# Weight sums of the output product's first half made one by one in earlier pairs and kept in DRAM

## The chip, the cores and the metric

The kernel runs on one core of a Trainium2 chip. The core has a matrix engine (TensorE, called PE in the profile; PEld is its weight load), a vector engine (VectorE, DVE), an activation engine (ScalarE, ACT), a general one (GpSimd, POOL) and a queue engine (SyncE, SP), which here issues nearly all transfers between DRAM and the on-chip buffers. Each engine runs its instructions in a fixed order and waits at each for what it needs.

The metric is device time in microseconds. The kernel before takes 1977.21 us, the median of three runs (1974.11 to 1977.57).

## The reference, cut to what matters

One decoder layer on 512 tokens of width 2048, in float32:

```python
h = rms_norm(x, norm1_g)
proj = h @ w_in                      # columns for two groups of heads
out_a = gla_mixer(...)               # 4 heads, chunked gated linear attention
out_b = dilated_mixer(...)           # 8 heads, dilated windows, QK-norm, T5 bias
mix = concatenate([out_a, out_b], -1)
x = x + mix @ w_out                  # the output product
h2 = rms_norm(x, norm2_g)
x = x + (silu(h2 @ w_gate) * (h2 @ w_up)) @ w_down
```

The change concerns how the weights of `mix @ w_out` are prepared, for the first 1024 of its 2048 columns.

## The kernel before

**Products by pairs.** Every large product is made in pairs of two 512-column blocks, `w1` and `w2`, for all 512 tokens. A pair splits the depth into four groups of 512 rows (three in the last down projections) and works by a scheme with seven products instead of eight (Winograd's form of Strassen's): the weights of a group come as four quarters of 256 rows by 512 columns, `a` and `c` from `w1`, `b` and `d` from `w2`. The seven products, in the order P1, P5, P6, P3, P7, P2, P4 (`PRODUCTS`), use `a`, `d` and `c` as they are (P1, P3, P2: `SINGLE`) and four sums: P5 is b - a, P6 is d minus that, P7 is d - b, P4 is c minus the P6 sum (`SUMS_OF`). The other operand has its own sums (A11, S1 and so on, made by `Operand.split` and the jobs around it).

**One item.** A product of one group is an item; a pair has 28. `stream` (the loop around lines 315 to 370) goes through the items of all pairs. For the item after the next, `Pair.source` gives the weights: a quarter loaded from DRAM (`load_quarter`, line 222), or a sum that DVE makes in place from two quarters (line 256). Each weight tile is then split in a high part `wh`, rounded by ACT (line 331), and a low part `wl`, the rest, made by DVE (line 335). PE does 12 matmuls an item (line 361): eight with `wh` against the operand's high and low parts, four with `wl`. Two buffers each hold `wh` and `wl`, twelve buffers of 512 KB hold weight quarters (tag `w`). A quarter in use for a later sum keeps its buffer; a load waits until one is free.

**Beside the items.** After the first eight matmuls of each item the pair's `step` runs some of the background: work written as generators, a piece at each `yield`. In the pairs of the input product these are the gates, the bias tables (a copy of 2.5 MB within DRAM, `rep_d`) and the attention heads, which read the projections back from DRAM. During the output product's first pair, `late_jobs` makes that product's remaining operand sums from `mix_d` (the mixers' output in DRAM): a load of 256 KB into one of the buffers T, v, qT, kT or r, a DVE subtraction or addition (lines 1242 to 1246) and a split (lines 174 and 175). `rate` and `paced` say how much a step runs.

**Order.** PE, ACT and DVE follow the order of the program in the first pair, which is written out by hand. In the others a planner orders the instructions of each engine, and the issues on SP's queue, by program order among those that its own estimate of time holds ready; so a sum may be placed ahead of the point at which it is written, where it expects DVE to be idle. What was placed is then fixed, and an instruction whose data come late holds up what stands behind it on its engine.

**The pairs in question.** The hand-ordered pair (`first_pair`) is pair 1. The list `pairs` holds the rest: pairs 2 to 5 are the input product's further columns (va1/va0, qb0/kb0, vb1/vb0, qb1/kb1), pair 6 the gate, pairs 7 and 8 the two halves of the output product (`opm`), then eleven pairs for the SwiGLU's inputs and six for its output.

The buffers with tag `r` (four of 256 KB, `rpool`) hold parts of x in pair 1 and are used again by the heads of the dilated mixer and by the operand jobs.

Of the kernel before, what the change touches and what calls it, by code (L numbers as in the profile page):

```python
# [10 lines left out]
F32 = mybir.dt.float32  # L11
# [3 lines left out]
ALU = mybir.AluOpType  # L15
# [3 lines left out]
P = 128  # L19
# [14 lines left out]
SINGLE = {"P1": "a", "P3": "d", "P2": "c"}  # L34
SUMS_OF = {"P5": "ba", "P6": "da", "P7": "db", "P4": "ca"}
# [72 lines left out]
def block_kernel(ctx: ExitStack, tc: tile.TileContext, ins, out):  # L108
# [127 lines left out]
    class Pair:  # L236


        def __init__(self, op, rows, w1, w2, final, step, scale=None, before=None):
            self.op, self.rows, self.w1, self.w2 = op, rows, w1, w2  # L240
            self.final, self.step, self.scale, self.before = final, step, scale, before
            self.q, self.dst, self.held = {}, {}, {}

        def quarter(self, name, g):
# [5 lines left out]
        def source(self, prod, g):  # L250

            if prod in SINGLE:
                return self.quarter(SINGLE[prod], g)
            one, two = SUMS_OF[prod]
            src = self.quarter(two, g)
            nc.vector.tensor_tensor(src, self.quarter(one, g), src, op=ALU.subtract)  # L256
            return src
# [50 lines left out]
        def end(self, prod):  # L308
            src = self.dst[prod]
            if prod in ("P1", "P5", "P6"):  # L310
                self.held[prod] = self.seeds(src, int(prod == "P5"))
            elif prod == "P4":
                later(1, lambda: self.final(1, 0, None, src), hold=True)
            else:
                which = {"P3": "P6", "P7": "P5", "P2": "P1"}[prod]
                self.close(self.held[which], src, *CLOSES[prod])

    def stream(pairs):

# [173 lines left out]
        later(1, lambda: close("d"), hold=True)  # L493

    background = []
    deferred = []

    def later(units, fn, hold=False):
# [22 lines left out]
    def finish(ready):  # L521

        while not ready():
            run_soon()
            try:
                next(background[0])
            except StopIteration:
                background.pop(0)

    def paced(counts):  # L530
        counts = iter(counts)
        return lambda: step(next(counts, 1))

    def rate(*stretches):


        owed = [0.0]
        rates = iter([r for n, r in stretches for _ in range(n)])

        def go():  # L540
            owed[0] += next(rates, stretches[-1][1])
            n = owed[0] if owed[0] > 0.3 else 0
            owed[0] = min(owed[0] - (step(n) or 0.0), 1.0)

        return go
# [546 lines left out]
    def final_proj(n1, n2):  # L1092
        def final(half, which, tiles, acc_):
            if tiles is None:
                tiles = emitted(acc_, lambda m: row_scale(half, m))
            name = (n1, n2)[which]
            dst = proj[name]
            for m in range(2):
                r = half * 256 + m * P
                put = lambda r=r, m=m: store(dst[r : r + P, :], tiles[m])  # L1100
                if name[:2] in ("qb", "kb"):
                    heads_norm(tiles[m], put)
                else:
# [184 lines left out]
    def pair(*args, **kw):  # L1288
        pairs.append(Pair(*args, **kw))

    pair(opx, rows_in, col(1536), col(1024), final_proj("va1", "va0"), rate((22, 1), (6, 0.6)),
         row_scale, before=lambda: background.extend([gates(), bias_tables()]))
    flow = rate((90, 0.41))
    pair(opx, rows_in, col(3088), col(4112), final_proj("qb0", "kb0"), flow, row_scale)
    pair(opx, rows_in, col(5648), col(5136), final_proj("vb1", "vb0"), flow, row_scale)
    pair(opx, rows_in, col(3600), col(4624), final_proj("qb1", "kb1"), flow, row_scale)
    pair(opx, rows_in, col(2048), col(2560), final_gate, rate((5, 0.6), (23, 1.05)), row_scale)


    rows_mix = [(1024 + 256 * g, 256 * order[g]) for g in range(4)]  # L1300
# [36 lines left out]
    def final_out(second):  # L1337
        rest_of = {}

        def ahead(half, which):  # L1340
            tok = 1 - half
            rest_of[half, which] = residual_loads(
                [2 * tok, 2 * tok + 1], 512 * (2 * second + which),
                lambda t, c: x[t * P : (t + 1) * P, c : c + 512],
            )

        def final(half, which, tiles, acc_):
            tok = 1 - half
            rows = [2 * tok, 2 * tok + 1]
            ch = 2 * second + which  # L1350
            tiles = residual(tiles, acc_, rest_of.pop((half, which)))
            for m in range(2):
                t = rows[m]
                store(x1_d[t][:, 512 * ch : 512 * ch + 512], tiles[m])
                jk = work("st", (P, DV), bufs=2).bitcast(mybir.dt.bfloat16)
                nc.scalar.activation(
                    jk, tiles[m], AF.Square, accum_out=ss2[:, t, ch : ch + 1]
                )
            if second:
                turn = scaled_store(tiles, rows, tok, xn_d[2 * ch : 2 * ch + 2], 4 * ch)  # L1360

                def rest():
                    turn()
                    if which == 1 and half == 1:
                        background.append(early_jobs(opn, (2, 3), tops, False))
                        background.append(late_jobs(opn, ((2, 3),), tops, bots, False))

                later(2, rest)
                if which == 0 and half == 1:
                    output_scales()  # L1370
            elif which == 0 and half == 1:
                nc.vector.tensor_tensor(part2, ss2[:, :, 0], ss2[:, :, 1], op=ALU.add)
# [35 lines left out]
        turn()  # L1408
        yield

    ocol = lambda c: w_out[:, c : c + 512]
# [190 lines left out]
```

## Time and profile before

| | us |
|---|---|
| median of three runs | 1977.21 |
| the profiled execution, device time | 1975.93 |
| its span (first to last instruction) | 1974.1 |
| PE busy | 1932.0 |
| DVE busy | 1655.0 |
| ACT busy | 1094.1 |

How to read it: the page gives for each engine its busy time, its share of the span and its instructions. A table of windows gives the same for stretches of the span, with the clock that PE was granted (1.00 is full), the mean busy share of the 16 DMA engines and what they moved. A timeline line has the start in us, the duration, the engine, the line of the kernel, the operation with what it writes and reads, the count of what was merged into the line, and in brackets the idle time of the engine before it with what ended it. Matmuls overlap, so a merged line's duration reaches into the next one's start; the pace is read from starts. A line of transfers gives their count, their size and the median time from issue to landing.

### The profile page before, as it was taken

Reading aid. Unit: us, or ns where it says so; the run is one execution under the profiler, and the core shown is the slowest. Engines: PE = TensorE matmul, PEld = TensorE weight load, DVE = VectorE, ACT = ScalarE, POOL = GpSimd, SP = SyncE. Lnnn points to the kernel's source line nnn. Section 1 sums busy time; section 2 is a strip of 40 time slices with the busy share of each in tenths; the row PEclk is TensorE's granted clock in tenths of the full one; section 3 lists DMA queues with packets and bytes.
Section 4 is the critical chain, followed back from the end, with each engine's and each line's share of the span. In section 5 each row is a group of like instructions: output and inputs, shape, how many; then the busy total and the mean of one; then the engine's idle time right before and its main releaser. Section 6 shows DMA issues by size and latency. Waiting matters only on the chain.

```text
span 1974.1 us, 25791 instructions
## 1 busy us (share of the span) xinstructions
PE 1932.0 (98%) x9226; PEld 1671.6 (85%) x9226; DVE 1655.0 (84%) x1850; ACT 1094.1 (55%) x1600; POOL 58.7 (3%) x81
## 2 busy tenths in 40 slices
PE   7999999999999999999999999999999999999998
PEld 6888888888878877888888888888888888888887
DVE  7997887868789789878878878878879989989987
ACT  6664564566766666545545545445446646546443
POOL 0000230010000000000000000000000000000000
PEclk9999999999999999999999999999999999999999
DMA  8358365374666685554554554554555855855762
GB/s 277 113 170 276 106 186 157 127 213 133 214 205 203 215 278 163 179 166 129 182 166 132 176 165 129 175 163 132 172 163 168 294 204 180 301 179 178 248 213 75
DMA packets 237113, 360.45 MB, mean 183 GB/s; under 512 B 18246, under 2 KB 96783, under 8 KB 236984
## 3 DMA queue, kind: packets, MB, share of 16 engines
q1 hardware_dynamic: 236776, 358.72, 57.3%
q8 instruction: 72, 1.18, 0.3%
q14 instruction: 57, 0.47, 0.1%
q10 hardware_dynamic: 208, 0.08, 0.0%
HBM read 296.59 MB, written 64.51 MB: 183 GB/s over the span
## 4 chain that ended last, share of the span: by engine, by line
PE 79%; DVE 8%; DMA 7%; issue 3%; ACT 2%; SPq 1%; POOL 1%; DVEq 0%; ACTq 0%
PE acc L361 71%; DVE wl L335 3%; PE acc L429 3%; DVE wa L256 1%; PE bank L1120 1%; PE bank L978 1%; ACT wh L331 1%; DMA wc<-in_w_in 1%; DVE AS L175 1%; DMA T<-p_d 1%; DMA x<-in_x 1%; DMA q<-y_d 0%; PE bank L1010 0%; DMA xn_d<-oT 0%; DVE seed L1325 0%
## 5 line engine op out<-in xcount | busy, mean ns | idle before, releaser
L361 PE MATMUL acc<-wh,AS 128*128 128x512 f32 x3008 | 712.0, 379 | 0.0
L361 PEld LDWEIGHTS acc<-wh,AS 128*128 128x128 f32 x3008 | 569.1, 189 | 81.7 <-ACT wh L331 0.6
L331 ACT CAST wh<-wa 128x1024 fp32r<-128x1024 f32 x376 | 393.6, 1048 | 384.2 <-PE acc L361 359.5
L361 PE MATMUL acc<-wh,AA 128*128 128x512 f32 x2256 | 536.4, 381 | 5.6 <-ACT wh L331 5.4
L335 DVE TENSOR_TENSOR wl<-wa,wh 128x1024 fp32r<-128x1024 f32 x376 | 457.4, 1220 | 72.0 <-ACT wh L331 46.5
L361 PEld LDWEIGHTS acc<-wh,AA 128*128 128x128 f32 x2256 | 426.7, 190 | 70.0 <-ACT wh L331 9.1
L361 PE MATMUL acc<-wl,AS 128*128 128x512 f32 x1504 | 395.7, 386 | 7.9 <-DVE wl L335 7.2
L361 PEld LDWEIGHTS acc<-wl,AS 128*128 128x128 f32 x1504 | 278.9, 189 | 61.7 <-DVE wl L335 20.9
L361 PE MATMUL acc<-wl,AA 128*128 128x512 f32 x1128 | 299.0, 388 | 6.1 <-DVE wl L335 6.1
L361 PEld LDWEIGHTS acc<-wl,AA 128*128 128x128 f32 x1128 | 210.7, 190 | 38.7 <-DVE wl L335 9.0
L331 ACT CAST wh<-wb 128x1024 fp32r<-128x1024 f32 x94 | 98.6, 1049 | 127.4 <-PE acc L361 122.7
L331 ACT CAST wh<-wc 128x1024 fp32r<-128x1024 f32 x94 | 98.4, 1047 | 106.8 <-PE acc L361 102.2
L331 ACT CAST wh<-wd 128x1024 fp32r<-128x1024 f32 x94 | 98.4, 1048 | 105.8 <-PE acc L361 102.3
L256 DVE TENSOR_TENSOR wa<-wc,wa 128x1024 f32<-128x1024 f32 x94 | 114.6, 1223 | 43.8 <-DMA wc<-in_w_gate 24.2
L335 DVE TENSOR_TENSOR wl<-wc,wh 128x1024 fp32r<-128x1024 f32 x94 | 114.8, 1221 | 38.6 <-ACT wh L331 38.6
L335 DVE TENSOR_TENSOR wl<-wd,wh 128x1024 fp32r<-128x1024 f32 x94 | 114.5, 1220 | 35.0 <-ACT wh L331 28.1
L335 DVE TENSOR_TENSOR wl<-wb,wh 128x1024 fp32r<-128x1024 f32 x94 | 113.9, 1219 | 6.1 <-ACT wh L331 6.1
L256 DVE TENSOR_TENSOR wb<-wd,wb 128x1024 f32<-128x1024 f32 x94 | 114.6, 1219 | 1.0 <-DMA wd<-in_w_in 0.5
L256 DVE TENSOR_TENSOR wa<-wb,wa 128x1024 f32<-128x1024 f32 x94 | 113.7, 1220 | 0.8
L256 DVE TENSOR_TENSOR wa<-wd,wa 128x1024 f32<-128x1024 f32 x94 | 113.1, 1218 | 0.1
L298 DVE SCALAR_TENSOR_TENSOR seed<-acc,rs,seed 128x512 f32<-128x512 f32 x96 | 70.5, 746 | 24.9 <-PE acc L361 24.9
L282 ACT ACTIVATE seed<-acc,rs 128x512 f32<-128x512 f32 x96 | 60.6, 681 | 1.4 <-PE acc L361 0.8
(289 smaller groups left out, 1367.4 us busy)
## 6 DMA issues: line engine op xcount, KB each, us to landing
wa<-in_w_gate SPq DMA_DIRECT2D x44, 512.0 KB, 4.4
wb<-in_w_up SPq DMA_DIRECT2D x44, 512.0 KB, 4.4
wd<-in_w_up SPq DMA_DIRECT2D x44, 512.0 KB, 4.5
wc<-in_w_gate SPq DMA_DIRECT2D x44, 512.0 KB, 3.6
wc<-in_w_in SPq DMA_DIRECT2D x28, 512.0 KB, 4.1
wa<-in_w_in SPq DMA_DIRECT2D x24, 512.0 KB, 5.2
wb<-in_w_in SPq DMA_DIRECT2D x24, 512.0 KB, 6.1
wd<-in_w_in SPq DMA_DIRECT2D x24, 512.0 KB, 6.0
```

The lines of the kernel that those rows point to most:

```text
L175: nc.vector.tensor_tensor(a[:, :, 1, :], src, a[:, :, 0, :].bitcast(F32), op=ALU.subtract)
L256: nc.vector.tensor_tensor(src, self.quarter(one, g), src, op=ALU.subtract)
L282: nc.scalar.activation(halves(t), unfolded(src[m]), AF.Copy, scale=self.scale(half, m))
L298: nc.vector.scalar_tensor_tensor(halves(seed[m]), unfolded(src[m]), self.scale(half, m), halves(seed[m]), op0=ALU.mult, op1=ALU.add,)
L331: nc.scalar.copy(high[k], sources[k])
L335: nc.vector.tensor_tensor(low[k], sources.pop(k), high[k].bitcast(F32), op=ALU.subtract)
L361: nc.tensor.matmul(p.dst[prod][m], a[:, jj, hl, m * P : (m + 1) * P], folded(w[:, jj, :]), start=fresh and g == 0 and len(terms) == 2 and ...
L429: recent["pe"] = nc.tensor.matmul(dst[prod][m], a[:, jj, hl, m * P : (m + 1) * P], folded(w[:, jj, :]), start=fresh and g == 0 and len(ter ...
L978: nc.tensor.matmul(lp[:, :n], qh[:, b * P : (b + 1) * P], kh[:, :n], start=True, stop=True)
L1120: nc.tensor.transpose(bk[:, jj, m * P : (m + 1) * P], tiles[m][:, f : f + P], ident)
```

## The change: sums from DRAM

A new generator, `weight_sums`, makes the four sums of pair 7 for each of its four groups, in halves of 128 rows: eight rounds. A round loads four parts of 128x512 (256 KB) into the `r` buffers, waits four steps, makes one subtraction in each of the next four steps, then stores four results to DRAM tiles (`out_sums`) and rests two steps. It is advanced by one piece in every step of pairs 2, 3 and 4 (`beside`), beside the background that these steps run anyhow. A round takes ten steps, the whole 80 of the 84 steps of these pairs.

In pair 7, `source` loads each sum as one tile of 512 KB. It has 28 weight loads instead of 16, seven a group instead of four, makes no sum on DVE and keeps no quarter past its own product.

```diff
@@ class Pair
+            self.sums = sums
@@ def source(self, prod, g)
             if prod in SINGLE:
-                return self.quarter(SINGLE[prod], g)
+                t = self.quarter(SINGLE[prod], g)
+                if self.sums:
+                    self.q.pop((SINGLE[prod], g))
+                return t
+            if self.sums:
+                t = wpool.tile([P, 2, 512], F32, name=nm("ws"), tag="w")
+                load(t, self.sums[prod, g])
+                return t
             one, two = SUMS_OF[prod]
...
+    def weight_sums(rows, w1, w2, sums):
+
+        tt = nc.vector.tensor_tensor
+
+        def fetch(g, j):
+            res = []
+            for name in "abdc":
+                r0 = rows[g][0 if name in "ab" else 1] + P * j
+                t = rpool.tile([P, 2, 256], F32, name=nm("r"), tag="r").rearrange(
+                    "p a b -> p (a b)")
+                load(t, (w1 if name in "ac" else w2)[r0 : r0 + P, :])
+                res.append(t)
+            return res
+
+        for g in range(4):
+            for j in range(2):
+                a, b, d, c = fetch(g, j)
+                for _ in range(4):
+                    yield
+                for dst, one, two in (
+                    (a, b, a), (b, d, b), (d, d, a), (c, c, d)
+                ):
+                    tt(dst, one, two, op=ALU.subtract)
+                    yield
+                for prod, t in (("P5", a), ("P7", b), ("P6", d), ("P4", c)):
+                    store(sums[prod, g][:, j, :], t)
+                yield
+                yield
...
+    aside = []
...
+    def side(units):
+
+        count = [0]
+
+        def go():
+            count[0] += 1
+            if aside and count[0] % units == 0:
+                try:
+                    next(aside[0])
+                except StopIteration:
+                    aside.pop(0)
+
+        return go
+
+    def both(*fns):
+        return lambda: [fn() for fn in fns]
...
+    ocol = lambda c: w_out[:, c : c + 512]
+    rows_mix = [(1024 + 256 * g, 256 * order[g]) for g in range(4)]
+    out_sums = {
+        (prod, g): dram([P, 2, 512], f"{prod}_{g}_d") for prod in SUMS_OF for g in range(4)
+    }
+    aside.append(weight_sums(rows_mix, ocol(0), ocol(512), out_sums))
+    beside = side(1)
-    pair(opx, rows_in, col(1536), col(1024), final_proj("va1", "va0"), rate((22, 1), (6, 0.6)),
+    pair(opx, rows_in, col(1536), col(1024), final_proj("va1", "va0"),
+         both(rate((22, 1), (6, 0.6)), beside),
          row_scale, before=lambda: background.extend([gates(), bias_tables()]))
     flow = rate((90, 0.41))
-    pair(opx, rows_in, col(3088), col(4112), final_proj("qb0", "kb0"), flow, row_scale)
-    pair(opx, rows_in, col(5648), col(5136), final_proj("vb1", "vb0"), flow, row_scale)
+    flowing = both(flow, beside)
+    pair(opx, rows_in, col(3088), col(4112), final_proj("qb0", "kb0"), flowing, row_scale)
+    pair(opx, rows_in, col(5648), col(5136), final_proj("vb1", "vb0"), flowing, row_scale)
     pair(opx, rows_in, col(3600), col(4624), final_proj("qb1", "kb1"), flow, row_scale)
...
-    pair(opm, rows_mix, ocol(0), ocol(512), final_out(0), paced([1] * 28),
+    pair(opm, rows_mix, ocol(0), ocol(512), final_out(0), paced([1] * 28), sums=out_sums,
          before=lambda: finish(lambda: ("S3", 3) in opm.t))
     pair(opm, rows_mix, ocol(1024), ocol(1536), final_out(1), rate((28, 1.2)))
```

More of the change, by code (lines that the diff above doesn't have):

```diff
@@ L236, in block_kernel, with __init__ @@
     class Pair:
-        def __init__(self, op, rows, w1, w2, final, step, scale=None, before=None):
+        def __init__(self, op, rows, w1, w2, final, step, scale=None, before=None, sums=None):
             self.op, self.rows, self.w1, self.w2 = op, rows, w1, w2
             self.final, self.step, self.scale, self.before = final, step, scale, before
+            self.sums = sums
             self.q, self.dst, self.held = {}, {}, {}
@@ L1289, in pair @@
         pairs.append(Pair(*args, **kw))
-    pair(opx, rows_in, col(1536), col(1024), final_proj("va1", "va0"), rate((22, 1), (6, 0.6)),
+    ocol = lambda c: w_out[:, c : c + 512]
[7 more added lines that the diff above has]
+         both(rate((22, 1), (6, 0.6)), beside),
          row_scale, before=lambda: background.extend([gates(), bias_tables()]))
     flow = rate((90, 0.41))
-    pair(opx, rows_in, col(3088), col(4112), final_proj("qb0", "kb0"), flow, row_scale)
-    pair(opx, rows_in, col(5648), col(5136), final_proj("vb1", "vb0"), flow, row_scale)
+    flowing = both(flow, beside)
+    pair(opx, rows_in, col(3088), col(4112), final_proj("qb0", "kb0"), flowing, row_scale)
+    pair(opx, rows_in, col(5648), col(5136), final_proj("vb1", "vb0"), flowing, row_scale)
     pair(opx, rows_in, col(3600), col(4624), final_proj("qb1", "kb1"), flow, row_scale)
     pair(opx, rows_in, col(2048), col(2560), final_gate, rate((5, 0.6), (23, 1.05)), row_scale)
-    rows_mix = [(1024 + 256 * g, 256 * order[g]) for g in range(4)]
     x1_d = [dram([P, D], f"x1_d{t}") for t in range(4)]
@@ L1409, in first_columns @@
         yield
-    ocol = lambda c: w_out[:, c : c + 512]
     def output_scales():
```

## The prediction

> **What bounds the kernel now.** I read the page first. TensorE (PE) is busy almost everywhere, so only those places matter where it waits; windows cut at the pair borders show them. Pair 1 is the hand-ordered one; pair 2 starts at 105 us, pair 3 at 188, pair 4 at 276, pair 7 (first half of the output product) runs from 564 to 649.
>
> ```profile
> span 1974.1 us, 25791 instructions
> PE 1932.0 (98%) x9226; PEld 1671.6 (85%) x9226; DVE 1655.0 (84%) x1850; ACT 1094.1 (55%) x1600; POOL 58.7 (3%) x81
> ```
>
> ```profile
> core 0: us, PE busy (x) PEld busy (x) DVE busy (x) ACT busy (x) POOL busy (x), PEclk, DMA share, GB/s
> 102.00:143.28 41.28, 40.13 (x183) 33.43 (x182) 40.32 (x43) 26.85 (x36) 0.53 (x1) 1.00 0.48 155
> 143.28:188.33 45.05, 45.05 (x226) 38.98 (x225) 32.79 (x38) 18.29 (x24) 0.56 (x3) 1.00 0.80 275
> 188.33:275.92 87.59, 87.51 (x438) 75.19 (x437) 69.44 (x83) 48.19 (x103) 23.17 (x26) 1.00 0.57 170
> 564.48:582.28 17.80, 14.58 (x58) 11.56 (x56) 16.84 (x21) 12.05 (x20) 0.00 (x0) 0.81 0.56 186
> 582.28:607.05 24.77, 22.06 (x98) 17.73 (x97) 24.72 (x30) 14.39 (x20) 0.00 (x0) 1.00 0.27 86
> 607.05:648.67 41.62, 41.62 (x194) 36.21 (x192) 40.49 (x46) 26.18 (x40) 0.00 (x0) 1.00 0.86 276
> ```
>
> The last three windows are pair 7: P1; P5 and P6; then P3, P7, P2 and P4. In P5 and P6 VectorE (DVE) works 24.72 of 24.77 us while PE has holes; in the last four products PE never stops although DVE is busy 40.49 of 41.62. So DVE sets the end in P5 and P6 alone. What it does there, over one item (a product of one group: 12 matmuls), and what PE does when it is free:
>
> ```profile
> 590.05 1.22 DVE L256 TENSOR_TENSOR wa<-wd,wa 128x1024 f32<-128x1024 f32 x1
> 591.19 0.69 DVE L175 TENSOR_TENSOR AS<-r,AS 128x512 fp32r<-128x512 f32 x1
> 591.79 1.22 DVE L335 TENSOR_TENSOR wl<-wa,wh 128x1024 fp32r<-128x1024 f32 x1
> 592.92 0.69 DVE L1244 TENSOR_TENSOR r<-r,kT 128x512 f32<-128x512 f32 x1
> 593.53 1.22 DVE L256 TENSOR_TENSOR wa<-wd,wa 128x1024 f32<-128x1024 f32 x1
> ```
>
> ```profile
> 607.05 1.89 PE L361 MATMUL acc<-wh,AS 128*128 128x512 f32 x8
> ...
> 609.64 1.89 PE L361 MATMUL acc<-wh,AS 128*128 128x512 f32 x8
> ```
>
> From sum to sum DVE needs 593.53 - 590.05 = 3.48 us an item, PE 609.64 - 607.05 = 2.59. By starts, a 128x1024 subtraction takes 591.19 - 590.05 = 1.14 us of DVE, a 128x512 one 591.79 - 591.19 = 0.60.
>
> **What the change removes: the 16 sums of pair 7 (L256).** In P5 and P6 an item's DVE work falls to 3.48 - 1.14 = 2.34 us, below 2.59, so PE sets the pace. Eight items then take 8 x 2.59 = 20.72 us instead of 24.77: a gain of 4.05. Low end 2.7, the idle time that the profile itself puts down to DVE:
>
> ```profile
> L361 PE MATMUL acc<-wl,AS 128*128 128x512 f32 x32 | 8.6, 392 | 2.7 <-DVE wl L335 2.7
> ```
>
> The P7 and P4 sums, 8 x 1.14 = 9.1 us, lie under a PE that is busy 41.62 of 41.62: nothing. The P1 window is slow for another reason: DVE waits there for an operand tile that makes a trip through DRAM, and the clock then drops.
>
> ```profile
> 570.00:580.00 10.00, 7.83 (x26) 5.99 (x27) 10.00 (x15) 9.44 (x16) 0.00 (x0) 0.66 0.53 175
> ```
>
> ```profile
> 571.20 2.08 PE L361 MATMUL acc<-wl,AA 128*128 128x512 f32 x4 [2.24 <-DVE wl L335]
> 574.25 3.78 PE L361 MATMUL acc<-wh,AA 128*128 128x512 f32 x8 [0.97 <-ACT wh L331]
> ```
>
> No sum stands between that wait and these matmuls, so I take nothing (bounds 0 and a gain of 1.1, one sum). The slow matmuls cost (2.08 - 1.03) + (3.78 - 1.89) = 2.9 us, with 1.03 and 1.89 the usual durations of four and eight; that price returns below.
>
> The Trainium skill, "TensorE: Matmul & The Clock Gate", section "Part 1: The HAM clock gate (the "warmup" mystery)", says that the array falls to half clock after an idle window of about 3.4 us. Here a hole of 2.24 us was enough, so the row decides; by the rule a short hole would cost only itself.
>
> **What it adds: 32 subtractions of 128x512 in pairs 2 to 4.** Each group has four, one after each of four steps; eight groups take 80 of the 84 steps. DVE pays 32 x 0.60 = 19.2 us and saves 16 x 1.14 = 18.2, so in total nothing moves; the place decides. In steps counted from 0, the subtractions lie at 4-7, 14-17 and 24-27 of pair 2, 6-9 and 16-19 of pair 3, across the border to pair 4, and at its 8-11 and 18-21.
>
> Pair 2, steps 4-7, about 115 to 126 us: DVE works 40.32 of 41.28 us from 102 to 143 and PE already waits for it twice.
>
> ```profile
> 129.73 1.13 PE L361 MATMUL acc<-wl,AS 128*128 128x512 f32 x4 [0.80 <-DVE wl L335]
> ...
> 135.53 1.13 PE L361 MATMUL acc<-wl,AS 128*128 128x512 f32 x4 [0.35 <-DVE wl L335]
> ```
>
> What is queued behind a subtraction is the low part wl (L335) of a coming item, which PE waits for. So four times 0.60 goes straight to the end: 2.4 (bounds 0, if they are placed elsewhere, and 2.4). Steps 14-17 and 24-27 fall in a stretch with 45.05 - 32.79 = 12.3 us of idle DVE and a full PE: nothing, and 4.8 without that cover.
>
> Pair 3, steps 6-9, 207 to 218 us:
>
> ```profile
> 210.92 1.23 DVE L256 TENSOR_TENSOR wa<-wd,wa 128x1024 f32<-128x1024 f32 x1
> 212.07 2.52 DVE L335 TENSOR_TENSOR wl<-wa,wh 128x1024 fp32r<-128x1024 f32 x2
> 215.25 0.42 DVE L866 SCALAR_TENSOR_TENSOR qT<-bank,L 128x256 f32<-128x256 f32 x1 [0.67 <-PE bank L858]
> ```
>
> DVE runs into an idle stretch at 215, so only part of 2.4 shows: I take 0.6, the rise of one step (bounds 0 and 2.4). Pair 4: the border steps and 8-11:
>
> ```profile
> 300.33 1.13 PE L361 MATMUL acc<-wl,AS 128*128 128x512 f32 x4 [0.94 <-DVE wl L335]
> 303.73 1.13 PE L361 MATMUL acc<-wl,AS 128*128 128x512 f32 x4 [0.55 <-DVE wl L335]
> ```
>
> ```profile
> 309.18 0.69 DVE L860 TENSOR_TENSOR T<-k,oT 128x512 f32<-128x512 f32 x1 [2.98 <-ACT oT L853]
> ```
>
> One or two of these subtractions stand ahead of the two late wl, the rest meets 2.98 us of idle DVE: 1.0 (bounds 0 and 4.8, eight of them).
>
> **What it adds: transfers.** 32 loads and 32 stores of 256 KB in pairs 2 to 4, and 28 - 16 = 12 more weight loads of 512 KB in pair 7. The first group's loads (1 MB) can go out before pair 2's second weights, whose wait is then DVE's first sum:
>
> ```profile
> 90.00:100.00 10.00, 10.00 (x49) 8.74 (x48) 10.00 (x11) 3.84 (x5) 0.00 (x0) 1.00 1.02 360
> ```
>
> ```profile
> L222 SPq DMA_DIRECT2D wb<-in_w_in x4: 367/490/644, 94.6 to 97.1; - x4
> L256 DVE TENSOR_TENSOR wa<-wb,wa x4: 1214/1222/1226, 105.2 to 116.2; 128x1024 f32<-128x1024 f32 x4
> ...
> DMA to landing us min/median/max: 5.7/6.3/6.8
> ```
>
> 1.05 MB at 360 GB/s is 2.9 us. The last of the four lands near 97.1 + 6.3 = 103.4, 1.8 us ahead of the first use, so I count 2.9 - 1.8 = 1.1 (bounds 0 and 2.9).
>
> All issues go through SP's one queue in order. A group's loads need the four r buffers, which its predecessor's stores still read, and come two steps after these stores, about 5.2 us. Behind a waiting load stand weight loads, stores, and the tiles of the attention heads, for which PE itself waits in its order.
>
> ```profile
> va<-seed SPq DMA_DIRECT2D x4, 256.0 KB, 10.8
> T<-ls_d SPq DMA_DIRECT2D x2, 64.0 KB, 3.3
> ```
>
> ```profile
> 164.10 0.93 SPq L829 DMA_DIRECT2D T<-ls_d  x2
> ```
>
> ```profile
> 168.08 0.61 PE L842 MATMUL bank<-mats,T 128*128 128x128 f32 x4
> ```
>
> Between 150 and 170 us a bias table is being copied, and stores took 10.8 us to land: the second group's stores (about 157) would land near 168, and a load that waits for them holds SP till then. T, if it stands behind, lands at 168 + 3.3 = 171.3, 3.2 us after PE wants it. Elsewhere weights come up to twelve buffers ahead, which covers some us. I take 1.0 (bounds 0 and 3.2; a stall that also drops the clock is a rival).
>
> The Trainium skill, "DMA: Bandwidth & Descriptors", section "Anatomy of one DMA — SWDGE (gpsimd) path", gives about 2.0 us plus bytes at 436 GB/s, stated for GpSimd's transfers. An estimate by that page for a group's 1.05 MB is 4.4 us, under the 5.2: by it SP never waits and the sum below is 1.0 smaller. The 10.8 us row speaks against it.
>
> Pair 7 has the room: in P5 and P6 the engines are busy 0.27, and each load is asked for twelve items early. 6.3 MB over the 42 us from 564 to 607 add 148 GB/s to 86 to 186. I take 0.5 for later landing of operand tiles (bounds 0 and 3.2, the lateness taken for T).
>
> **Sum.** -4.05 + 2.4 + 0.6 + 1.0 + 1.1 + 1.0 + 0.5 = +2.55 us. The span becomes 1974.1 + 2.6 = 1976.7, the profiled execution 1975.93 + 2.6 = 1978.5. The median of the runs is 1977.21, 1.3 above that execution, so I forecast 1979.8: the gain is paid back. All terms at their good ends give 1977.2 - 5.2 = 1972; at their bad ends -2.7 + 2.4 + 2.4 + 4.8 + 2.9 + 3.2 + 3.2 = +16.2, or 1993.
>
> **Rivals.** *The cost is hidden.* The subtractions are placed where DVE idles (12.3 us in the second part of pair 2), and the full 4.05 with up to one more us in P1 stays: 1972.5. For it: PE waits for DVE in these pairs for under 3 us in all. Against it: 40.32 of 41.28. *SP holds a head's tile.* One mechanism: T (L829) stands behind a load that waits for a landing store; it decides once that store lands later than 164.8 us, 3.3 before PE's 168.08. Price 3.2 and the slow clock 2.9 on top of the sum, less the 1.0 in it: 1979.8 + 5.1 = 1984.9, and near 1990 if another place does the same. For it: 10.8 us; against it: the order on SP isn't known. *Pair 7 turns to its loads.* The operand tiles come behind 512 KB each, and DVE waits for those as long as it did for sums: the 4.05 is lost, 1979.8 + 4.1 = 1983.9. Against it: share 0.27. *It doesn't do what it says*: if the sums were not done 200 us ahead of pair 7, this would wait; 80 of 84 steps leave pairs 5 and 6 between: under 1 in 100, left out.
>
> **How the numbers follow.** A difference under 0.2% (4 us) can't be told from no change here. Forecast 0.42 (1976 to 1984: no change 0.25, slower 0.17). Hidden 0.28 (faster 0.23, no change 0.05). SP 0.22 and loads 0.08, both slower. So faster 0.23, no change 0.30, slower 0.47; the range 1971 to 1989 leaves out the fastest of the second case and the worst of the third.
>
> **What would show it.** The last three windows again: if P5 and P6 of pair 7 take about 20.7 us with idle DVE, the gain is there; if PE waits for wl there, or DVE for a DMA, it isn't. PE's idle time before wl between 115 and 136 us should rise from 1.15 to about 3.5. Idle time of PE ahead of L842, or of DVE in a subtraction that waits for its load, would show the queue. I am wrong if pairs 2 to 4 keep their lengths, or if holes show in pairs 5, 6 or 8, which I take as unchanged.

## The result and the profile after

The changed kernel takes 1991.82 us, the median of four runs (1989.62 to 1995.65), beside 1976.38 for the kernel before on the same chip: a ratio of 1.0085, 95% interval 1.0072 to 1.0099. It is slower by 15 us. The prediction was 1979.8, with a range up to 1989: the sign of its sum was right, the size was not, and the time lies outside the range.

The first lines of the page of the profiled execution after the change:

```profile
span 1987.9 us, 25935 instructions
PE 1934.9 (97%) x9226; PEld 1674.1 (84%) x9226; DVE 1655.9 (83%) x1866; ACT 1094.6 (55%) x1600; POOL 56.3 (3%) x81
```

DVE has 16 instructions more (32 halves for 16 wholes) and the same busy time, as predicted. PE is busy 2.9 us longer, but the span is 13.8 us longer: most of the loss is time in which PE stands. To place it, both traces are cut where PE begins P5 of each pair from 2 to 8, which gives six windows. Before:

```profile
115.99:200.42 84.43, 83.28 (x398) 70.77 (x397) 70.25 (x80) 43.70 (x60) 4.50 (x7) 1.00 0.60 201
200.42:288.00 87.58, 87.50 (x437) 75.18 (x436) 69.70 (x86) 50.85 (x119) 25.67 (x27) 1.00 0.51 148
288.00:375.18 87.18, 85.69 (x423) 74.19 (x422) 65.69 (x82) 41.93 (x63) 6.64 (x9) 1.00 0.55 169
375.18:470.40 95.22, 95.22 (x499) 82.86 (x497) 74.18 (x115) 63.77 (x163) 11.33 (x16) 1.00 0.52 158
470.40:582.28 111.88, 106.39 (x554) 90.45 (x552) 87.25 (x146) 77.20 (x150) 0.00 (x0) 0.97 0.63 198
582.28:662.88 80.60, 75.55 (x346) 63.70 (x344) 77.17 (x88) 47.10 (x69) 2.96 (x2) 1.00 0.65 212
```

And after, with pair 7's P5 and P6 alone in the last row:

```profile
113.83:205.47 91.64, 85.95 (x398) 72.06 (x397) 77.01 (x93) 43.77 (x60) 3.17 (x7) 0.96 0.76 244
205.47:304.14 98.67, 91.98 (x437) 77.11 (x436) 79.40 (x102) 50.92 (x119) 24.16 (x27) 0.97 0.78 244
304.14:394.35 90.21, 87.10 (x422) 75.37 (x421) 67.72 (x84) 41.91 (x63) 7.09 (x10) 0.98 0.53 165
394.35:489.57 95.22, 95.22 (x498) 82.86 (x497) 74.21 (x115) 63.77 (x163) 11.32 (x16) 1.00 0.53 158
489.57:602.76 113.19, 106.33 (x553) 90.53 (x552) 84.82 (x145) 77.32 (x150) 0.00 (x0) 0.97 0.65 211
602.76:678.66 75.90, 73.88 (x345) 64.14 (x344) 63.55 (x73) 48.16 (x70) 2.96 (x2) 1.00 0.86 284
...
602.76:623.48 20.72, 20.72 (x97) 18.14 (x96) 20.19 (x27) 16.16 (x24) 0.00 (x0) 1.00 0.93 313
```

The first three windows grow by 7.21, 11.09 and 3.03 us, 21.3 together; the next two by 0 and 1.31. The last shrinks by 4.70, of which 24.77 - 20.72 = 4.05 is in P5 and P6, to the hundredth what was forecast. So the gain of P5 and P6 is all there; the cost in pairs 2 to 4 is what was mis-sized. In these three windows PE's idle time (length less busy) grows from 2.7 to 15.5 us, and its busy time by 8.6 us for the same matmuls, at a clock of 0.96 to 0.98 (the column after POOL).

The idle time is not spread; PE's timeline between 113 and 330 us shows these holes of over 1 us:

```profile
171.93 1.22 PE L398 MATMUL acc<-wh,AA 128*128 128x512 f32 x2 [5.12 <-ACT wh L368]
...
241.92 1.13 PE L398 MATMUL acc<-wl,AS 128*128 128x512 f32 x4 [1.23 <-DVE wl L372]
254.90 2.07 PE L398 MATMUL acc<-wl,AS 128*128 128x512 f32 x4 [3.22 <-DVE wl L372]
284.72 1.20 PE L398 MATMUL acc<-wl,AA 128*128 128x512 f32 x4 [1.94 <-DVE wl L372]
...
316.04 1.78 PE L398 MATMUL acc<-wl,AS 128*128 128x512 f32 x4 [3.11 <-DVE wl L372]
```

They are 14.6 of the 15.5 us. What makes the first hole is read from the timeline of SP's queue. Before, the weight load that matters went out right after the first two stores of `va`:

```profile
154.51 0.43 SPq L222 DMA_DIRECT2D wc<-in_w_in  x1
```

After:

```profile
145.48 0.72 SPq L674 DMA_DIRECT2D rep_d<-bias_d  x1
150.22 2.36 SPq L1155 DMA_DIRECT2D va<-seed  x2
152.64 0.74 SPq L351 DMA_DIRECT2D P_d<-r  x1
153.43 11.90 SPq L336 DMA_DIRECT2D r<-in_w_out  x4
165.43 0.38 SPq L222 DMA_DIRECT2D wc<-in_w_in  x1
```

The planner put the third group's four loads right behind the last store of the second group, since that store frees their buffer. A duration of 11.90 us for four issues is SP standing. The chain of waits says for what:

```profile
152.64 12.34 DMA P_d<-r
...
165.43 5.30 DMA wc<-in_w_in
...
170.83 1.05 ACT wh L368
...
171.93 1.22 PE acc L398 x2
```

The store needs 12.34 us to land behind the 2.5 MB bias copy; the load waits for it, the weight load waits for SP, ACT for the weights and PE for ACT. SP's waits from 95 to 360 us (total, times, longest) have two lines that the kernel before can't have:

```profile
SPq L351 <- DVE r L348: 25.0, 9, 6.3
SPq L336 <- DMA P_d<-r: 20.9, 9, 8.4
```

Stores wait for subtractions and loads for landed stores, 46 us in all. But the sum of SP's waits is no measure of the cost: added up over all rows of that view it is 193.7 us before and 169.7 after. For one, weight loads stand less for a free buffer (the first row is before, the second after):

```profile
SPq L222 <- DVE wl L335: 63.9, 31, 14.8
SPq L222 <- DVE wl L372: 40.2, 19, 17.1
```

What counts is which wait stands ahead of something that PE needs soon.

The other four holes aren't all of this kind. Ahead of 241.92 DVE stands 1.33 us at a subtraction whose load has not landed. Ahead of 254.90 DVE waits three times for weight quarters (1.22, 0.86 and 2.38 us, from 241.9 to 251.0), and stores and loads of the sums stand in the chain. Ahead of 284.72 DVE again stands at a subtraction for its load, 3.37 us. In the 17 us of the chain ahead of 316.04 no transfer of the sums appears, only pieces of an attention head on GpSimd, ACT and DVE and its store `ong_d`.

### The profile page after: what moved, and what is told of

The parts are those of the page before. It is cut to its first block, busy times and chain, and to the rows that moved or that the text cites. A ratio compares the mean times of both kernels' runs of the same rounds, so it can differ in the third digit from the quotient of the medians.

```text
span 1987.9 us, 25935 instructions
## 1 busy us (share of the span) xinstructions
PE 1934.9 (97%) x9226; PEld 1674.1 (84%) x9226; DVE 1655.9 (83%) x1866; ACT 1094.6 (55%) x1600; POOL 56.3 (3%) x81
## 4 chain that ended last, share of the span: by engine, by line
PE 72%; DMA 7%; DVE 7%; issue 3%; ACT 2%; POOL 1%; SPq 0%; DVEq 0%; ACTq 0%; POOLq 0%
PE acc L398 69%; DVE wl L372 3%; PE bank L1175 1%; DMA P_d<-r 1%; DVE wa L264 1%; ACT wh L368 1%; DMA wc<-in_w_in 1%; DMA xn_d<-oT 1%; DMA r<-in_w_out 1%; DMA wd<-in_w_in 1%; PE bank L1033 1%; DMA kT<-mix_d 0%; DVE AS L175 0%; DMA r<-xn_d 0%; PE bank L1065 0%
## 5 line engine op out<-in xcount | busy, mean ns | idle before, releaser
L368 ACT CAST wh<-wa 128x1024 fp32r<-128x1024 f32 x364 | 381.3, 1048 | 386.2 <-PE acc L398 361.4
L372 DVE TENSOR_TENSOR wl<-wa,wh 128x1024 fp32r<-128x1024 f32 x364 | 442.7, 1219 | 71.3 <-ACT wh L368 45.6
L368 ACT CAST wh<-wb 128x1024 fp32r<-128x1024 f32 x90 | 94.3, 1048 | 127.3 <-PE acc L398 117.2
L264 DVE TENSOR_TENSOR wa<-wc,wa 128x1024 f32<-128x1024 f32 x90 | 109.7, 1222 | 43.4 <-DMA wc<-in_w_gate 24.9
L372 DVE TENSOR_TENSOR wl<-wb,wh 128x1024 fp32r<-128x1024 f32 x90 | 108.8, 1217 | 3.6 <-ACT wh L368 3.4
L264 DVE TENSOR_TENSOR wb<-wd,wb 128x1024 f32<-128x1024 f32 x90 | 109.6, 1218 | 0.4
L264 DVE TENSOR_TENSOR wa<-wd,wa 128x1024 f32<-128x1024 f32 x90 | 108.2, 1218 | 1.2 <-DMA wd<-in_w_in 1.1
L264 DVE TENSOR_TENSOR wa<-wb,wa 128x1024 f32<-128x1024 f32 x90 | 108.6, 1219 | 0.6
```

The costliest lines, as they stand in the source:

```text
L368: nc.scalar.copy(high[k], sources[k])
L372: nc.vector.tensor_tensor(low[k], sources.pop(k), high[k].bitcast(F32), op=ALU.subtract)
```

## The experiments

Every kernel was run beside the kernel before on its own chip; a ratio is to that. The first four take the change apart, the others move its instructions. The text on record calls "theory SP" that SP's one queue stands and holds up weight loads, "theory traffic" that the bytes delay other transfers, "theory DVE" that the subtractions' time or their waits in order on DVE cost; in made_not_stored and subtract_only these are theories 1, 2 and 3.

**The cost alone and the gain alone.** made_only takes away only pair 7's use of the sums:

```diff
-    pair(opm, rows_mix, ocol(0), ocol(512), final_out(0), paced([1] * 28), sums=out_sums,
+    pair(opm, rows_mix, ocol(0), ocol(512), final_out(0), paced([1] * 28),
```

used_only takes away `aside`, and in pair 7 loads a quarter where a sum would be:

```diff
-    aside.append(weight_sums(rows_mix, ocol(0), ocol(512), out_sums))
...
-                t = wpool.tile([P, 2, 512], F32, name=nm("ws"), tag="w")
-                load(t, self.sums[prod, g])
-                return t
+                one, two = SUMS_OF[prod]
+                return load_quarter(self.rows, two, g, self.w1 if two in "ac" else self.w2)
```

> The sums are made and stored as in the change, but pair 7 makes its own sums from its quarters as before; the stored ones are not read. If the cost lies in pairs 2 to 4 and pair 7 gains what its windows show (P5 and P6 in 20.7 us instead of 24.8), the time is the changed kernel's 1991.8 plus 4 to 5, so 1995 to 1997. If pair 7's 12 additional loads cost something too, it is below 1992.

> Pair 7 has 28 weight loads and no sums, as in the change, but nothing is made ahead: it loads a plain quarter where a sum belongs, so the sums are left out of the computation. All theories: pairs 2 to 6 as before and pair 7 about 4 us shorter, 1971 to 1973. If more loads in pair 7 cost as much as they bring, 1976.

made_only: 1996.93, ratio 1.0102 (1.0085 to 1.0120), +21.2 us. used_only: 1971.4, ratio 0.9977 (0.9965 to 0.9988), -4.3. Both lie where they were expected. Together +16.9, near the 15.4 of the whole change: the two parts don't act on each other much, and all that follows is about the making.

**Without the stores, and without most transfers.** made_not_stored drops the 32 stores, with pair 7 as in used_only. subtract_only loads four tiles once and makes all 32 subtractions on them, without stores and with pair 7 as in used_only.

```diff
-                for prod, t in (("P5", a), ("P7", b), ("P6", d), ("P4", c)):
-                    store(sums[prod, g][:, j, :], t)
```

```diff
+        kept = fetch(0, 0)
...
-                a, b, d, c = fetch(g, j)
+                a, b, d, c = kept
```

> Loads and 32 subtractions in pairs 2 to 4 as in the change, but no stores; pair 7 loads plain quarters, so the sums are left out of its products. Theory 1 (SP stands at loads that wait until a store has landed, and at stores that wait for a subtraction): nearly all of the cost goes, 1972 to 1978. Theory 2 (16.8 MB more traffic delays all transfers): half of the traffic is left, and half of the 20 us cost, about 1982. Theory 3 (DVE: the subtractions and their waits for loads): the cost stays, 1988 or more.

> Only the first round's four loads, then 32 subtractions on these same four tiles in the same steps, no stores; pair 7 loads plain quarters, so the sums are left out of its products. Theories 1 and 2: DVE's 19 us hide, 1971 to 1974. Theory 3, and my prediction's terms for DVE (2.4 + 0.6 + 1.0): 1976 and more.

made_not_stored: 1976.19, 1.0002 (0.9991 to 1.0013), as theory SP (1972 to 1978) had it. Against used_only the loads and subtractions cost 0.0025 of 1976, 4.9 us; the stores make the other 16.4 (1.0085 - 1.0002). The 4.9 lie in the second window, which was 87.58 before:

```profile
198.59:291.38 92.79, 88.47 (x438) 74.92 (x437) 79.96 (x103) 50.84 (x119) 32.58 (x27) 1.00 0.62 192
```

subtract_only: 1984.82, 1.0040 (1.0025 to 1.0055). By its number that is theory DVE (1976 and more), but its trace shows that it tests something else. The first row is DVE's timeline, the second PE's:

```profile
165.40 13.25 DVE L348 TENSOR_TENSOR r<-r,r 128x512 f32<-128x512 f32 x19
```

```profile
180.98 2.07 PE L396 MATMUL acc<-wl,AA 128*128 128x512 f32 x4 [10.11 <-DVE wl L370]
```

With nothing to wait for, the planner put 19 of the 32 subtractions in one block ahead of a `wl`, and PE stood 10.11 us. The yields of the generator don't hold an instruction to its step; only its data do. The other 13 subtractions left no hole over 1 us. What the subtractions alone cost at the places that they have in the change stays untested.

**The bytes alone.** copies_only has no tile and no subtraction: 32 copies of 256 KB from the weights to the same DRAM tensors, each held to the matmul of its step.

```diff
+                for prod, name in (("P5", "a"), ("P7", "b"), ("P6", "d"), ("P4", "c")):
+                    r0 = rows[g][0 if name in "ab" else 1] + P * j
+                    behind_now(store(
+                        sums[prod, g][:, j, :], (w1 if name in "ac" else w2)[r0 : r0 + P, :]))
+                    yield
```

> Leaves the making of the sums out: 32 copies of 256 KB from the weights straight to the same DRAM tensors, from SP's queue, four in a row of steps and eight groups of them over pairs 2 to 4, each held to the matmul of its step; no tile, no subtraction, no wait for a landing store. Pair 7 loads a plain quarter of weights in place of each sum, as in the run that showed the gain alone (1971.4). Theory traffic: 8.4 MB read and 8.4 MB written in the same stretch as in the change, so most of the 15.6 us that the stores cost stays: 1982 to 1990. Theory SP: nothing stands, 1971 to 1976.

1977.05, 1.0004 (0.9995 to 1.0013): 5.3 us over used_only, between the two expectations. Traffic by itself is a real but small part. It lies in the second window too (first row), and there at one place, where copies issued right ahead make a weight load of 512 KB land in 8.24 us (second row, the chain), and PE waits (third row, its timeline):

```profile
200.83:292.93 92.10, 88.12 (x438) 75.02 (x436) 71.02 (x88) 50.39 (x119) 29.59 (x27) 1.00 0.59 183
```

```profile
236.86 8.24 DMA wc<-in_w_in
```

```profile
248.33 1.13 PE L392 MATMUL acc<-wl,AS 128*128 128x512 f32 x4 [2.96 <-DVE wl L366]
```

**Other queues.** from_gpsimd issues the sums' loads and stores from GpSimd's queue, loads_from_gpsimd the loads alone.

```diff
-                load(t, (w1 if name in "ac" else w2)[r0 : r0 + P, :])
+                nc.gpsimd.dma_start(t, (w1 if name in "ac" else w2)[r0 : r0 + P, :])
...
-                    store(sums[prod, g][:, j, :], t)
+                    nc.gpsimd.dma_start(sums[prod, g][:, j, :], t)
```

> The change with the 32 loads and 32 stores of the weight sums issued from GpSimd's queue instead of SP's; bytes, subtractions and pair 7 as in the change. Theory SP (SP's one queue stands at loads that wait for a landing store and at stores that wait for a subtraction, and weight loads behind come late): with SP free nearly all of the cost of making the sums goes, and the gain in pair 7 stays: 1971 to 1979 us, PE holes before wl and wh in pairs 2 to 4 under 4 us in all, and no SP wait for a weight-sum load or store. Theory traffic (16.8 MB more delay whatever else lands): the bytes are the same, so 1986 to 1996. Theory DVE (subtractions that stand in order on DVE and wait for their loads): the loads come as late as before, DVE stands as long, 1984 to 1994.

> The change with only the 32 loads of the weight sums issued from GpSimd's queue; the stores stay on SP's. Theory SP, landing part (what costs is SP standing at a load until the store that frees its buffer has landed, 20.9 us over nine places in the trace after the change): 1973 to 1982. Theory SP, both parts alike (the stores that wait for subtractions hold SP for another 25.0 us over nine places): half of the cost stays, 1980 to 1987. Theory traffic and theory DVE: 1986 to 1996, as the change.

from_gpsimd: 2024.39, 1.0240 (1.0224 to 1.0255); loads_from_gpsimd: 1997.98, 1.0106 (1.0091 to 1.0121). Both lie above what any theory gave them. Theory SP as stated falls here: SP no longer stood at a load of the sums, and it got worse. PE's largest hole in from_gpsimd, and what DVE waited for between 95 and 400 us:

```profile
222.00 2.07 PE L398 MATMUL acc<-wl,AA 128*128 128x512 f32 x4 [41.23 <-DVE wl L372]
```

```profile
DVE r L348 <- DMA r<-in_w_out: 30.8, 9, 9.5
```

The planner put five groups close together on DVE, from 174.7 to 219.7 us. At the head of each DVE stood until the group's loads had come; these were issued behind the last group's stores and took 3.6 to 4.5 us to land, and behind the subtractions stood the low part that PE needed. So the wait seems to be in the circle of load, subtraction, store and landing through four buffers, and it falls on whichever in-order engine meets a piece too early. The theory became: the queue's order at single places, SP's or DVE's.

**Held to their steps.** loads_held ties each load to the matmul of its step (three steps between loads and subtractions, three after the stores); all_pinned ties loads, subtractions and stores (steps 0, 4 and 5, 6); all_pinned_gpsimd does so with GpSimd's queue.

```diff
+    def behind_now(made):
+        if "pe" in now:
+            tc.add_manual_dep(
+                made.ins, now["pe"].name,
+                mybir.DependencyInfo(mybir.DependencyClass.NoSync, mybir.DependencyReason.DATA),
+                reason="now",
+            )
```

> The change with each load of a weight sum held behind the matmul of the step at which the generator asks for it, so that the planner can't put it right behind the store that frees its buffer; three steps between loads and subtractions and three between stores and the next loads. Same bytes, same queue. Theory SP: SP stands shorter, a load comes some 7.8 us after its group's stores, where landings took 5.6 in the middle and 12.3 at most; the stall at the bias table is mostly left (its store landed 12.3 us after issue), the others go: 1975 to 1986. Theory traffic and theory DVE: 1986 to 1996.

> The change with loads, subtractions and stores each held behind the matmul of their own step: loads at step 0 of a group, two subtractions at steps 4 and 5 each, stores at step 6, the next loads at step 10. Queue SP as in the change. The last look showed that the cost moves with the in-order engine that meets a group too early: SP stood 25.0 and 20.9 us in the change, 30.6 at the stores when loads alone were held, and DVE stood 41.2 us at one place when GpSimd's queue issued the transfers and the groups were put close together. Theory queue order (what costs is an in-order queue, SP's or DVE's, that meets one of these instructions before its partner is done): with all three kinds held the stores find their subtractions done and the loads come 10 us after the stores, so holes in pairs 2 to 4 shrink to some 5 us: 1973 to 1982. Theory traffic (copies alone cost 5.6 over the run with the gain alone) gives its part in any case, which is the low end's 1977. Theory that it costs the same wherever the waits are (DVE's time, 19.2 us in pairs 2 to 4): 1985 to 1992.

> As the kernel with loads, subtractions and stores held to their steps, and both kinds of transfers issued from GpSimd's queue. Theory queue order: SP meets nothing of the sums and DVE meets its subtractions late enough, so neither stands: 1972 to 1979, and without the 41.2 us hole of the unheld version. If GpSimd's transfers are slower in themselves or delay the others: 1985 or more. Theory DVE's time: 1985 to 1992.

loads_held: 1988.13, 1.0058 (1.0041 to 1.0075), above what theory SP gave it and within the 1986 to 1996 of the other two. all_pinned: 1983.28, 1.0045 (1.0028 to 1.0061), just above its expectation. all_pinned_gpsimd: 1991.55, 1.0083 (1.0068 to 1.0098), far above the 1972 to 1979 of theory queue order and within what the rivals gave. Holding helps in part only, since it also moves what isn't held. In all_pinned_gpsimd nothing of the sums stood on SP, but two weight loads came behind the stores of `ong_d`, at 204.77 us; in the kernel before, no weight load is issued between 195 and 217 us, so they had all gone out earlier. The rival that GpSimd's transfers delay the others isn't excluded: the loads into `wb` and `wd` landed after 8.6 and 8.7 us in the median here, after 5.6 and 5.7 in all_pinned. DVE's row:

```profile
213.39 2.52 DVE L264 TENSOR_TENSOR wa<-wb,wa 128x1024 f32<-128x1024 f32 x2 [6.03 <-DMA wb<-in_w_in]
```

**One group moved.** third_group_late is the change with the third group asked for four steps later and its loads held; all later groups follow four steps later too. Up to the bias table SP's order is the change's.

```diff
+                if (g, j) == (1, 0):
+                    for _ in range(4):
+                        yield
+                now["hold"] = (g, j) == (1, 0)
```

> The change with one group moved: the third group's four loads are asked for four steps later and held to that step's matmul, so that on SP's queue the weight load that stood behind them in the change, the two stores of v and T come first; the queue up to there is the change's, entry for entry. Theory SP (the 11.9 us that SP stood at these loads made that weight load late, PE's 5.12 us hole at 171.9 and the slow clock behind it): this hole goes, the start of P5 in pair 3 comes 5 to 8 us earlier against its place before (from +5.1 to between -2 and 0), and what the later groups cost stays or moves: 1982 to 1988. Theory that the standing at this place is not what costs (traffic at the bias table, DVE's subtractions): the hole stays within 2 us, start of P5 of pair 3 at +3 or more, 1989 to 1995.

1981.79, 1.0030 (1.0020 to 1.0039): 10.9 us better than the change by the ratios and just under the 1982 to 1988 that theory SP gave it. SP's rows at the place, PE's row and the first window again:

```profile
154.52 0.74 SPq L365 DMA_DIRECT2D P_d<-r  x1
155.31 0.74 SPq L222 DMA_DIRECT2D wc<-in_w_in  x1
...
174.93 0.42 SPq L346 DMA_DIRECT2D r<-in_w_out  x1
```

```profile
169.55 0.70 PE L412 MATMUL acc<-wh,AA 128*128 128x512 f32 x2 [1.36 <-ACT wh L382]
```

```profile
115.45:200.91 85.46, 83.74 (x399) 70.61 (x398) 72.66 (x87) 43.71 (x60) 3.85 (x7) 1.00 0.75 248
```

The weight load goes out at 155.31 instead of 165.43, the hole falls from 5.12 to 1.36 us, and the window from 91.64 to 85.46, 1.0 above before. The bias copy, its traffic and the subtractions are all still there. The cause of this place is shown: the standing of SP ahead of a weight load. This place is worth these 6.2 us; the other 4.7 of the 10.9 come later, where all groups had moved. Pair 3's window stays long, at 97.58. And SP stood no less at the instructions of the sums, 49.2 us at stores and 7.1 at loads: the place of a wait decides, not the sum. The start of pair 3's P5 came at +0.5 instead of the -2 to 0 expected.

**Half the sums.** Only P5 and P6 gained, so half_sums makes only their sums ahead (24 loads, 16 subtractions, 16 stores); P7 and P4 are summed in pair 7 as before. half_sums_pinned holds them all to their steps. half_sums_mixed leaves the first three groups to the planner, which had done well there, and holds the other five, all in the spacing of half_sums_pinned.

```diff
-            if self.sums:
+            if self.sums and prod in ("P5", "P6"):
                 t = wpool.tile([P, 2, 512], F32, name=nm("ws"), tag="w")
                 load(t, self.sums[prod, g])
+                if prod == "P6":
+                    self.q["a", g] = t
                 return t
```

```diff
-        if "pe" in now:
+        if now.get("hold"):
...
+                now["hold"] = 2 * g + j >= 3
                 a, b, d = fetch(g, j)
```

> Only the sums of P5 and P6, the two products in which pair 7 gained, are made ahead: 24 loads, 16 subtractions and 16 stores instead of 32 of each, three of the four r buffers a group, ten steps a group as in the change; pair 7 makes P7's and P4's sums itself, as before the change, under a PE that was busy all the time there, and loads six tiles a group. Theory queue order: the gain stays (P5 and P6 near 20.7 us) and half of the instructions can stand, with one buffer free for the next group's first load: 8 to 12 of the 21.2 us cost are left, 1978 to 1986. Theory that the first standing place (11.9 us at the bias table) decides whatever the count: 1984 to 1990. Below 1971 it would beat both kernels.

> The same half with loads, subtractions and stores held to steps 0, 5, 7 of ten. Theory queue order: about half of what the fully pinned kernel still cost (13.4 over the gain alone, by 1983.3 against 1974.2 and a gain of 4.3): some 7 less the gain, 1972 to 1979. Theory traffic: half of 5.6 remains in any case. If the planner's order of the other SP transfers decides and not the count of held ones: 1980 to 1986.

> The kernel that makes only the sums of P5 and P6 ahead, with its first three groups left to the planner, as in the version that showed no hole in pair 2, and the other five held to steps 0, 5 and 7 of ten, as in the version that showed only 1.1 and 0.5 us of holes from pair 3 on. Theory queue order (each hole belongs to a place in the queue and not to the number of instructions): both holes, 4.0 us near 173 and 3.3 us near 237, are gone and the gain of about 4 in pair 7 shows: 1970 to 1974, faster than both kernels. Theory that another place stands instead as soon as one is mended: 1975 to 1981.

half_sums: 1976.33, 1.0004 (0.9995 to 1.0014), below the 1978 to 1986 expected. half_sums_pinned: 1976.46, 1.0001 (0.9991 to 1.0011), as expected. Equal times, and each has one large hole, at another place (PE's rows of the one and of the other):

```profile
237.33 2.08 PE L399 MATMUL acc<-wl,AS 128*128 128x512 f32 x4 [3.25 <-DVE wl L373]
```

```profile
172.86 1.11 PE L409 MATMUL acc<-wh,AA 128*128 128x512 f32 x2 [4.01 <-ACT wh L379]
```

half_sums_mixed, built to have neither: 1971.2, 0.9978 (0.9968 to 0.9988), faster than both kernels, as theory queue order said. Its windows:

```profile
114.12:199.45 85.33, 83.81 (x398) 70.53 (x397) 73.61 (x86) 43.62 (x60) 4.08 (x7) 1.00 0.70 233
199.45:289.08 89.63, 87.93 (x438) 75.10 (x436) 72.08 (x91) 50.66 (x119) 26.15 (x27) 1.00 0.61 193
...
585.30:662.22 76.92, 74.62 (x346) 64.68 (x345) 71.76 (x81) 48.23 (x71) 2.96 (x2) 0.99 0.79 253
```

Pairs 2 and 3 cost 0.9 and 2.1 us more than before, P5 of pair 7 to P5 of pair 8 takes 3.7 less, and SP has no wait for a landing store among its waits from 95 to 360 us. The whole gain rests on the medians: the profiled execution took 1973.97, 2.8 above the median, and its six windows together are 548.1 us beside 546.9 before, since the one ahead of pair 7's P5 took 113.85 (111.88 before). Which group is held was chosen from the two other traces, so it fits this kernel's order and no other.

## Why the prediction was wrong

*The gain: right.* P5 and P6 take 20.72 us, PE busy 20.72 of it. used_only has the same 4.3 in all.

*The first megabyte (1.1): nothing.* Pair 2's P5 began at 113.83, earlier than the 115.99 before; it lies between 113.8 and 115.7 in all the changed kernels, with this load or without.

*Pair 2, steps 4 to 7 (2.4): nothing.* The window of the prediction, after:

```profile
102.00:143.28 41.28, 40.71 (x184) 33.69 (x183) 41.19 (x46) 26.22 (x34) 0.38 (x1) 1.00 0.68 209
143.28:188.33 45.05, 39.94 (x191) 33.69 (x191) 33.38 (x42) 14.39 (x16) 0.39 (x2) 0.92 0.80 261
```

DVE has three instructions more in the first stretch, though six subtractions lie in it, and four more in the second: others gave way into the idle half, and PE lost nothing: its idle time before wl from 115 to 136 us, which was to rise from 1.15 to 3.5, fell to 0.36. The rival *the cost is hidden* was right for this term. The terms for pairs 3 and 4 (0.6 and 1.0) can't be told from the holes there: made_not_stored, loads and subtractions together, loses 5.2 us in the window of pair 3 and none in that of pair 4.

*SP and its landings (1.0, bounds 0 and 3.2): the step that failed.* The prediction had the mechanism, the place and nearly the time: a store to land near 168 behind the bias table, a load that holds SP till then. It landed at 164.98. Four things in the step were wrong. What stood behind was put down as T, because PE waits for T by name; the load that hurt was a weight quarter, which was excused with "weights come up to twelve buffers ahead". It was issued 10.9 us later than before, and the twelve buffers covered only about half of that. The four loads were to come two steps, 5.2 us, behind the stores; the planner put them 0.8 us behind (152.64 and 153.43). The price, 3.2, was one hole without the clock; the first window cost 7.2. And it was taken as one place, while SP stood nine times at loads and nine times at stores: pairs 2 to 4 cost 21.3 us where all terms for them, with the 1.1, came to 6.1. That SP's standing made most of the 7.2 (6.2) is shown by third_group_late, that the stores are needed for 16.4 of the loss by made_not_stored; how much of the rest is SP's and how much DVE's own standing isn't. The rival *SP holds a head's tile* had the right kind of event with the wrong tile; "near 1990 if another place does the same" came closest to 1991.8, and got too little weight.

Beside that term stood, not followed, the estimate by the Trainium skill, "DMA: Bandwidth & Descriptors", section "Anatomy of one DMA — SWDGE (gpsimd) path": 4.4 us for a group, so that SP never waits. The trace disagrees: these stores of 256 KB landed after 2.0 to 12.3 us, and SP waited 20.9 us for them.

*Pair 7's operand tiles (0.5): 1.3,* in the window from pair 6's P5 to pair 7's; used_only has 1.15 there (113.03). But third_group_late, with the same loads in pair 7, takes 110.66, less than the kernel before, so that these loads cost anything there isn't shown.

*Sum.* By the windows: 7.2 + 11.1 + 3.0 + 1.3 - 4.7 = 17.9 where the prediction had +2.55. Less 2.2 for the earlier start of pair 2's P5 that is 15.8 at pair 8's; 2.0 of it came back by the end of the span, which was not followed up. What stays open is how pair 3's 11.1 us divide: copies_only shows 4.5 there for bytes alone (92.10 - 87.58), made_not_stored 5.2 without a store, and the two overlap in the same late weight loads.

## What to carry to other kernels

An extra stream of loads and stores on a queue that others use is priced first by what stands behind its waiting instructions: list the entries behind each one that waits for a landing, and how late each may be. Here the bytes alone cost 5.3 us and loads with subtractions 4.9, of some 20, and the queue's waits in all even fell. A circle of load, compute and store through few buffers cost time in every arrangement of all 32 sums that was tried; moving it to another queue moved the wait. Half of the sums, with the first three groups placed by the planner and the rest held, took nearly all of it away. Make ahead only what is on the path at the place of use: half of the sums had all of the gain in P5 and P6.

## What the runs showed of the hardware

A 256 KB store took 12.34 us to land behind a 2.5 MB copy within DRAM, and 2.0 at best. PE's clock fell behind some holes and not behind others as long. Behind the 3.11 and 3.22 us above the next four matmuls took 1.78 and 2.07 us, as the 2.24 in the prediction's rows left 2.08. Behind the 1.94 they took 1.20, but the eight that followed 3.55 instead of 1.89 (first row, after). Behind 2.96 in copies_only and 3.48 in loads_from_gpsimd (second row) four took 1.13, no more than behind the 1.23:

```profile
285.71 3.55 PE L398 MATMUL acc<-wh,AA 128*128 128x512 f32 x8
```

```profile
246.68 1.13 PE L398 MATMUL acc<-wl,AS 128*128 128x512 f32 x4 [3.48 <-DVE wl L372]
```

So the length of a single hole doesn't decide it, and what does stays open. The Trainium skill, "TensorE: Matmul & The Clock Gate", section "Part 1: The HAM clock gate (the "warmup" mystery)", has about 3.4 us of idle; in these rows 1.94 was enough and 3.48 was not.
